# One PSUM bank for each half product of a Winograd stage in a two-layer encoder trunk

## The chip, the cores and the metric

The kernel runs on one core of one Trainium2 chip. The metric is the device time of one execution in microseconds. Five engines work side by side, each through its own instructions in order: TensorE (PE, with its weight loads shown apart as PEld), VectorE (DVE), ScalarE (ACT), GpSimd (POOL) and SyncE (SP), which issues all loads and stores here. They wait for each other through semaphores. On-chip data lies in SBUF; TensorE writes its products to PSUM, and a result is read from there by VectorE or ScalarE.

## The reference

Two layers; sequence and model width are 1024, everything is float32:

```
for l in range(DEPTH):                                   # DEPTH = 2
    h = rms_norm(x, pre_norm_g[l])
    aq, ak, av, ag, bq, bk, bv, bg = split(h @ w_in[l])  # 512,512,512,512,512,128,128,512 columns
    oa = diff_attention(aq, ak, av, lam, rel_bias)       # 4 heads, two softmaxes each, T5 bias
    ya = rms_norm(oa, diff_subln_g[l]) * (1 - lam_init) * silu(ag)
    q, k = rope(rms_norm(bq)), rope(rms_norm(bk))
    ob = gqa_attention(q, k, bv)                         # 8 query heads, 2 key/value heads of 64
    yb = ob * silu(bg)
    y = concatenate([ya, yb]) @ w_out[l]
    x = x + rms_norm(y, post_norm_g[l])
```

## The kernel before, in words

Every large product is made of three products of reduced precision: a float32 operand is split into a high part (a rounding cast, on ScalarE) and a low part (the operand less its high part, on VectorE), and high·high, high·low and low·high are added up in PSUM. "Low part" below always means that subtraction.

A layer goes through these stages. (1) The keys, values and queries of group B, then the values of group A, in chunks of token tiles (`tok_chunk`), whose results alternate between a bank of the tag `pO` and one of `pS`. In layer 0, `line` also makes the rows of the T5 bias in between, four evictions of 4x512. (2) The Winograd stage (`wino_steps`, L471 to L549): the four 512-column chunks AK, AG, BG and AQ are each computed as a 2x2 block product with seven half-size products in place of eight. `sum_steps` makes the sums of blocks of h (s1 to s4), `loads` brings four 512 KB pieces of the weight per chunk, `preps` makes the weight's seven blocks and splits them into parts. A product `i` is run in two halves `cb` of 128 columns by `run(i, cb)`: twelve matmuls of 512 columns into one PSUM bank. The list `plan` says for each product its PSUM group, which block of h it takes, whether it opens the group (`first`) or adds to what is there, and what is read from the bank afterwards: a copy to `y` tiles, an addition (`added`) of the bank to a `y` tile, or a `post` that scales, splits and stores the result (`post_parts`) or applies SiLU and stores it (`post_gate`). The kept `y` sums are called s1, u2 and u3. (3) Attention, in ticks (`tick`, L754): in each one set of scores is reduced by VectorE and exponentiated by ScalarE, the next set is computed by TensorE, older probabilities are transposed, and a piece of an older product with V is done. The last chunk's products 5 and 6 are left out of the stage and run in the first five ticks as fillers (`FILL`, L32; `fill_part`). (4) The ending (after the last scores, order `ENDING`): the remaining parts of attention, the conversions of the output weight, and the first two gated, transposed y tiles (`y_transposed`, L1009). (5) The out-projection in two halves of 512 columns, with y tiles 2 to 7 transposed on the way; then the post norm and the residual. Group A's attention is normalised on GpSimd, which also has low parts of probabilities and weights.

PSUM has eight banks: the tag `pS` has two tiles of two banks, `pT` and `pO` two tiles of one bank each. What an instruction waits for is found tile by tile: a matmul into a tile waits for every earlier reader of that tile, whichever half it read.

What sets the order: during the Winograd stage only TensorE keeps the program's order, and a scheduler places the instructions of the other engines; in attention and its ending TensorE, VectorE, ScalarE and GpSimd all keep the program's order, and SP's is the scheduler's.

In the stage before, groups a and b have one two-bank tile of `pS` for both halves, and group c one bank of `pO` for each half, in which product 6 adds to product 5. Three products lie in b (s2, s3, a22) and two in c (s1, s4).

Of the kernel before, what the change touches and what calls it, by code (L numbers as in the profile page):

```python
# [17 lines left out]
P = 128  # L18
# [35 lines left out]
def hybrid_encoder(ctx, tc, x, rel_bias, pre_norm_g, w_in, diff_lambda, diff_subln_g,  # L54
# [58 lines left out]
    def ps_o():  # L113
        return ps.tile([P, 512], F32, tag="O", name=nm("pO"), bufs=2)
# [4 lines left out]
    def f(t):  # L119
        return t.bitcast(F32)  # L120
# [105 lines left out]
    def build_bias_rows():  # L226
# [18 lines left out]
        def line(j):  # L245
            lt = e_tile()
            for i in range(2):
                pl = ps_o()
                sl = slice(i * 512, i * 512 + 512)
                pe.matmul(pl[:4], parts, ohs[j][:64, sl], start=True, stop=True)  # L250
                dve.tensor_scalar(lt[:4, sl], pl[:4], -1.0, None, ALU.mult)
# [53 lines left out]
    def layer(l, hT, ends, given):  # L305
# [164 lines left out]

        def wino_steps(c0, post):  # L471

# [19 lines left out]
            def t4():  # L492
                dve.tensor_tensor(raw[1, 0], raw[1, 0], raw[0, 0], ALU.subtract)
                parted(4, raw[1, 0])
# [3 lines left out]
            preps = [lambda: parted(0, raw[0, 0]), lambda: parted(1, raw[1, 0]), t3,  # L498
                     lambda: parted(3, raw["t3"]), t4, lambda: parted(5, raw[0, 1]), lambda: parted(6, raw[1, 1])]

            def bank(grp, cb):
                if grp == "c":
                    if (grp, cb) not in ps_:
                        ps_[grp, cb] = ps_o()
                    return ps_[grp, cb]
                if grp not in ps_:
                    ps_[grp] = ps_s()
                return ps_[grp][:, cb * 512:cb * 512 + 512]

# [24 lines left out]
            def done(cb, th, src):  # L534
# [5 lines left out]
                    ("b", "s3", False, lambda cb: added("b", "u3", "s1", cb) and None),  # L540
                    ("b", "a22", False, lambda cb: done(cb, 1, added("b", "s1", "s1", cb))),
                    ("c", "s1", True, lambda cb: done(2 + cb, 1, added("c", "u3", "u3", cb))),
                    ("c", "s4", False, lambda cb: done(2 + cb, 0, added("c", "u2", "u2", cb)))]

# [119 lines left out]
        else:  # L664
# [12 lines left out]
        chunks = [wino_steps(C_AK, post_parts(1.0, store_k)), wino_steps(C_AG, post_gate(0)),  # L677
                  wino_steps(C_BG, post_gate(1)), wino_steps(C_AQ, post_parts(-0.125, store_q))]
        loads = [fn for c in chunks for fn in c[0]]
# [7 lines left out]
        for n in range(7 * len(chunks)):  # L687
            if n < 2:
                late[n]()
            if n + WLD < len(loads):  # L690
                loads[n + WLD]()
            if n + WPR < len(preps):
                preps[n + WPR]()
            if n == 21:
                warm = s_tile()
                inorder[:] = [nc.scalar]
                act.activation(warm, neglam, AF.Exp)
                inorder[:] = [nc.tensor]
            if n < 26:
# [309 lines left out]
        def y_transposed(t):  # L1009
# [5 lines left out]
            for kh in range(2):  # L1015
# [7 lines left out]
                else:  # L1023
                    dve.tensor_tensor(gate[:, sl, :], pT, gate[:, sl, :], ALU.mult)
                split(yT[0][:, sl, :], yT[1][:, sl, :], gate[:, sl, :])
            return yT
# [214 lines left out]
```

## Time and profile before

| what | us |
|---|---|
| three runs | 1520.82, 1524.74, 1525.21 |
| median | 1524.74 |
| profiled execution | 1518.82 |
| its span | 1517.0 |
| PE, PEld busy | 1411.8, 1214.3 |
| DVE, ACT, POOL busy | 1051.1, 835.1, 662.2 |

The mean granted clock of TensorE was 0.992. Nearly all instructions are recorded through one helper, so all have line 67; they are told apart by tiles, such as `pS` or `y`. In a row of a timeline stand the start, the length, the engine, the line, the operation, what is written `<-` what is read, the count, and in brackets the idle time before it and the instruction that ended it. In a row of groups stand the total busy time and the mean length in ns, then the idle time before and its releasers.

### The profile page before, as it was taken

What the parts mean: (1) busy time and instruction counts of PE and PEld (TensorE: products, weight loads), DVE (VectorE), ACT (ScalarE), POOL (GpSimd) and SP (SyncE); (2) the same over time, 40 slices, a digit from 0 to 9 for tenths busy, and PEclk for the clock granted to TensorE, in tenths of its full rate; (3) what the DMA queues carried; (4) which work ended last, traced back from release to release, by engine and by line L of the source; (5) the groups of instructions that cost most, each with busy time, mean ns of one, the idle gap of its engine ahead of it and who ended that gap; (6) DMA issues with size and microseconds to landing.
All of it is one profiled execution on the core that took longest, in us unless ns stands there. A gap on an engine that the chain in (4) does not pass through costs nothing. (4 is left out here: it accounts for less than half of the span.)

```text
span 1517.0 us, 22632 instructions
## 1 busy us (share of the span) xinstructions
PE 1411.8 (93%) x8108; PEld 1214.3 (80%) x8108; DVE 1051.1 (69%) x1844; ACT 835.1 (55%) x1584; POOL 662.2 (44%) x708
## 2 busy tenths in 40 slices
PE   6999888888999999989999998888899999999998
PEld 6886666667999999978788876666689999998787
DVE  7869534447888888873786785434588888888624
ACT  5324233327888888853442242223488888888421
POOL 3520000006888888862233100000178888888321
PEclk9999999999999999999999999999999999999999
DMA  5467433177232323142534553224743242322223
GB/s 210 136 162 218 160 122 111 50 212 187 78 85 76 102 63 105 57 139 83 177 104 119 138 162 123 93 91 112 217 117 103 64 130 64 92 84 69 99 73 135
DMA packets 134609, 179.12 MB, mean 118 GB/s; under 512 B 10072, under 2 KB 98392, under 8 KB 132192
## 3 DMA queue, kind: packets, MB, share of 16 engines
q1 hardware_dynamic: 134496, 177.67, 38.7%
q8 instruction: 64, 1.05, 0.3%
q14 instruction: 49, 0.40, 0.1%
HBM read 120.98 MB, written 60.85 MB: 120 GB/s over the span
## 5 line engine op out<-in xcount | busy, mean ns | idle before, releaser
L67 PE MATMUL pO<-w,h 128*128 128x256 f32 (+1 forms) x3160 | 550.0, 322 | 0.0
L67 PEld LDWEIGHTS pO<-w,h 128*128 128x128 f32 x3160 | 486.2, 189 | 64.1 <-DVE y L67 0.5
L67 POOL TENSOR_SCALAR e<-e,s 128x1024 f32<-128x1024 f32 x64 | 72.1, 1127 | 559.4 <-DVE s L67 312.1
L67 PE MATMUL pS<-h,h 128*128 128x512 f32 x1024 | 295.7, 411 | 2.4 <-DVE s L67 2.4
L67 PE MATMUL pS<-h,w 128*128 128x512 f32 x768 | 189.9, 398 | 46.3 <-DVE y L67 24.0
L67 PEld LDWEIGHTS pS<-h,w 128*128 128x128 f32 x768 | 140.4, 188 | 94.5 <-DVE y L67 29.0
L67 PE MATMUL pT<-identr,e 128*128 128x128 f32 x1536 | 203.2, 275 | 7.2 <-DVE w L67 7.2
L67 PEld LDWEIGHTS pS<-h,h 128*128 128x128 f32 x1024 | 175.8, 191 | 26.5 <-issue 2.8
L67 DVE TENSOR_TENSOR w<-pT,w 128x512 fp32r<-128x512 f32 x256 | 170.1, 685 | 29.9 <-ACT w L67 29.8
L67 PEld LDWEIGHTS pT<-identr,e 128*128 128x128 f32 x1536 | 175.6, 142 | 11.4 <-issue 7.6
L67 POOL TENSOR_TENSOR w<-e,w 128x512 fp32r<-128x512 f32 x128 | 165.9, 1296 | 10.4
L67 ACT CAST w<-pT 128x512 fp32r<-128x512 f32 x256 | 143.9, 588 | 40.9 <-PE pT L67 38.0
L67 POOL TENSOR_TENSOR s<-s,mhalf 128x2 f32<-128x2 f32 (+2 forms) x96 | 85.4, 890 | 185.3 <-DVE s L67 182.0
L67 DVE TENSOR_REDUCE s<-pS 128x1 f32<-128x1024 f32 x128 | 156.3, 1221 | 10.0 <-PE pS L67 9.2
L67 ACT ACTIVATE e<-e,s 128x1024 f32<-128x1024 f32 x128 | 148.2, 1158 | 26.4 <-DVE s L67 25.7
L67 DVE CUSTOM_DVE_ANT_0 e<-pS,h 128x1024 f32<-128x1024 f32 x128 | 155.6, 1217 | 9.3 <-POOL e L67 4.4
L67 POOL TENSOR_TENSOR e<-e,e 128x1024 f32<-128x1024 f32 x64 | 153.3, 2395 | 5.3
L67 ACT ACTIVATE e<-pS,s 128x1024 f32<-128x1024 f32 x128 | 144.5, 1129 | 9.3 <-DMA h<-bq_d 5.7
L67 PE MATMUL pS<-w,h 128*128 128x512 f32 (+1 forms) x576 | 120.6, 367 | 0.0
L67 PEld LDWEIGHTS pS<-w,h 128*128 128x128 f32 x576 | 98.3, 198 | 15.5 <-issue 0.5
L67 ACT ACTIVATE e<-y 128x512 fp32r<-128x512 f32 (+2 forms) x64 | 47.3, 739 | 104.5 <-DVE y L67 77.3
L67 ACT ACTIVATE o<-pO 128x128 f32<-128x128 f32 (+2 forms) x97 | 37.0, 382 | 104.5 <-PE pO L67 93.7
(98 smaller groups left out, 1623.7 us busy)
## 6 DMA issues: line engine op xcount, KB each, us to landing
h<-aq_d SPq DMA_DIRECT2D x64, 256.0 KB, 4.3
h<-in_w_in_dram SPq DMA_DIRECT2D x20, 512.0 KB, 4.7
bq_d<-y SPq DMA_DIRECT2D x64, 128.0 KB, 2.4
av_d<-e SPq DMA_DIRECT2D x32, 256.0 KB, 2.4
e<-in_w_in_dram SPq DMA_DIRECT2D x16, 512.0 KB, 4.2
y<-in_w_in_dram SPq DMA_DIRECT2D x16, 512.0 KB, 5.2
ak_d<-e SPq DMA_DIRECT2D x32, 256.0 KB, 2.0
gate_d<-e SPq DMA_DIRECT2D x32, 256.0 KB, 2.0
```

Of the source, the lines that this page charges most:

```text
L67: ins = fn(*args, **kw)
```

## The change

Four edits. In `line`, the four evictions of 4x512 are done by ScalarE, with the scale −1, in place of VectorE. In `wino_steps` each pair of group and half has a tile of one bank: a in `pT`, b in `pS`, c in `pO`, and two new groups d and e for the products a22 and s4, in `pT` and `pS`, or for the last chunk (`tail`) both in `pO`. Products a22 and s4 each open their own group, s1 is alone in c, and what they shared in a bank is now put together on `y` tiles by one more addition per half and chunk. The order of the products is a11, a12, s2, s3, s1, a22, s4 (before: a22 ahead of s1), the weight blocks are prepared in that order, and the additions of a22 and s4 are put off to their post. So the last chunk's fillers are a22 and s4, and its last product within the stage is s1. In `y_transposed` the low parts of the y tiles are made by GpSimd, after both gate multiplications, in place of VectorE.

```
--- before.py
+++ after.py
@@ -248,7 +248,7 @@
                 pl = ps_o()
                 sl = slice(i * 512, i * 512 + 512)
                 pe.matmul(pl[:4], parts, ohs[j][:64, sl], start=True, stop=True)
-                dve.tensor_scalar(lt[:4, sl], pl[:4], -1.0, None, ALU.mult)
+                act.activation(lt[:4, sl], pl[:4], AF.Copy, scale=-1.0)
             nc.sync.dma_start(line_d[:, j * 1024:j * 1024 + 1024], lt[:4])
             if j:
                 for h in range(4):
@@ -468,7 +468,7 @@
             return [lambda: whole("s3", a21), lambda: whole("s2", a11), s1, s3s2, lambda: (s4(), parted("s2", h_tile)),
                     lambda: parted("s3", w_tile)], [lambda: parted("s1", h_tile), lambda: parted("s4", w_tile)]
 
-        def wino_steps(c0, post):
+        def wino_steps(c0, post, tail=False):
 
             raw, wb, ps_, snap = {}, {}, {}, {}
 
@@ -491,21 +491,20 @@
 
             def t4():
                 dve.tensor_tensor(raw[1, 0], raw[1, 0], raw[0, 0], ALU.subtract)
-                parted(4, raw[1, 0])
+                parted(5, raw[1, 0])
 
             loads = [lambda: load(0, 0, e_tile), lambda: load(1, 0, e_tile),
                      lambda: (load(1, 1, y_tile), load(0, 1, y_tile))] + [lambda: None] * 4
             preps = [lambda: parted(0, raw[0, 0]), lambda: parted(1, raw[1, 0]), t3,
-                     lambda: parted(3, raw["t3"]), t4, lambda: parted(5, raw[0, 1]), lambda: parted(6, raw[1, 1])]
+                     lambda: parted(3, raw["t3"]), lambda: parted(4, raw[0, 1]), t4, lambda: parted(6, raw[1, 1])]
+
+            homes = {"a": ps_t, "b": lambda: ps_s((P, 512)), "c": ps_o, "d": ps_o if tail else ps_t,
+                     "e": ps_o if tail else lambda: ps_s((P, 512))}
 
             def bank(grp, cb):
-                if grp == "c":
-                    if (grp, cb) not in ps_:
-                        ps_[grp, cb] = ps_o()
-                    return ps_[grp, cb]
-                if grp not in ps_:
-                    ps_[grp] = ps_s()
-                return ps_[grp][:, cb * 512:cb * 512 + 512]
+                if (grp, cb) not in ps_:
+                    ps_[grp, cb] = homes[grp]()
+                return ps_[grp, cb]
 
             def kept(name, cb):
                 if name not in snap:
@@ -538,9 +537,10 @@
                     ("a", "a12", False, lambda cb: done(cb, 0, bank("a", cb))),
                     ("b", "s2", True, lambda cb: added("b", "u2", "s1", cb) and None),
                     ("b", "s3", False, lambda cb: added("b", "u3", "s1", cb) and None),
-                    ("b", "a22", False, lambda cb: done(cb, 1, added("b", "s1", "s1", cb))),
-                    ("c", "s1", True, lambda cb: done(2 + cb, 1, added("c", "u3", "u3", cb))),
-                    ("c", "s4", False, lambda cb: done(2 + cb, 0, added("c", "u2", "u2", cb)))]
+                    ("c", "s1", True, lambda cb: (added("c", "u2", "u2", cb),
+                                                  done(2 + cb, 1, added("c", "s1", "u3", cb)))[1]),
+                    ("d", "a22", True, lambda cb: lambda: post(cb, 1, added("d", "u3", "u3", cb))),
+                    ("e", "s4", True, lambda cb: lambda: post(2 + cb, 0, added("e", "u2", "u2", cb)))]
 
             def run(i, cb, ks=range(4)):
                 mm(i, cb, ks)
@@ -675,7 +675,7 @@
         inorder[:] = [nc.tensor]
         early, late = sum_steps()
         chunks = [wino_steps(C_AK, post_parts(1.0, store_k)), wino_steps(C_AG, post_gate(0)),
-                  wino_steps(C_BG, post_gate(1)), wino_steps(C_AQ, post_parts(-0.125, store_q))]
+                  wino_steps(C_BG, post_gate(1)), wino_steps(C_AQ, post_parts(-0.125, store_q), True)]
         loads = [fn for c in chunks for fn in c[0]]
         preps = [fn for c in chunks for fn in c[1]]
         side = {j: [fn] for j, fn in enumerate(early)}
@@ -696,7 +696,7 @@
                 inorder[:] = [nc.scalar]
                 act.activation(warm, neglam, AF.Exp)
                 inorder[:] = [nc.tensor]
-            if n < 26:
+            if n < 7 * len(chunks) - 2:
                 for cb in range(2):
                     more = chunks[n // 7][2](n % 7, cb)
                     follow()
@@ -1022,7 +1022,10 @@
                     dve.scalar_tensor_tensor(gate[:, sl, :], pT, gsub, gate[:, sl, :], ALU.mult, ALU.mult)
                 else:
                     dve.tensor_tensor(gate[:, sl, :], pT, gate[:, sl, :], ALU.mult)
-                split(yT[0][:, sl, :], yT[1][:, sl, :], gate[:, sl, :])
+                act.copy(yT[0][:, sl, :], gate[:, sl, :])
+            for kh in range(2):
+                sl = slice(kh * 4, kh * 4 + 4)
+                gps.tensor_tensor(yT[1][:, sl, :], gate[:, sl, :], f(yT[0])[:, sl, :], ALU.subtract)
             return yT
 
         inorder[:] = [getattr(nc, n) for n in ORD]
```

Three places of the order. First TensorE in the AK chunk of layer 0, at the end of the first half of product s2 (`h209` and `h210` are the parts of s2, `w231` the weight block), its second half and the start of s3 (`w218`, `w219`). Before:

```order
L67 MATMUL pS240_1563<-h209_1347,w231_1485 128x512
L67 MATMUL pS240_1563<-h209_1347,w231_1485 128x512 [waits DVE_49]
L67 MATMUL pS240_1563<-h210_1348,w231_1485 128x512
L67 MATMUL pS240_1563<-h209_1347,w231_1485 128x512 x2
L67 MATMUL pS240_1563<-h210_1348,w231_1485 128x512
L67 MATMUL pS240_1563<-h209_1347,w231_1485 128x512 x2
L67 MATMUL pS240_1563<-h210_1348,w231_1485 128x512
L67 MATMUL pS240_1563<-h209_1347,w231_1485 128x512 x2
L67 MATMUL pS240_1563<-h210_1348,w231_1485 128x512
L67 MATMUL pS240_1563<-h209_1347,w231_1485 128x512
L67 MATMUL pS240_1563<-w218_1399,w236_1522 128x512 [waits DVE_49]
L67 MATMUL pS240_1563<-w219_1400,w236_1522 128x512
```

Now:

```order
L67 MATMUL pS241_1563<-h210_1348,w231_1485 128x512
L67 MATMUL pS241_1563<-h209_1347,w231_1485 128x512
L67 MATMUL pS243_1578<-h209_1347,w231_1485 128x512
L67 MATMUL pS243_1578<-h210_1348,w231_1485 128x512
L67 MATMUL pS243_1578<-h209_1347,w231_1485 128x512 x2
L67 MATMUL pS243_1578<-h210_1348,w231_1485 128x512
L67 MATMUL pS243_1578<-h209_1347,w231_1485 128x512 x2
L67 MATMUL pS243_1578<-h210_1348,w231_1485 128x512
L67 MATMUL pS243_1578<-h209_1347,w231_1485 128x512 x2
L67 MATMUL pS243_1578<-h210_1348,w231_1485 128x512
L67 MATMUL pS243_1578<-h209_1347,w231_1485 128x512
L67 MATMUL pS241_1563<-w218_1399,w237_1523 128x512 [waits DVE_49]
```

Before, the second half of s2 stood in the same tile and waited for VectorE's addition of the first half to `y`, and s3 waited for that of the second half. Now the second half is in a tile of its own and waits for nothing; s3's first half waits for the addition of s2's first half, a block earlier.

Second, SP between the end of the stage and the start of attention in layer 0: L943 and L946 load keys of group A and the bias, L964 loads the keys of group B (`bk_d`), L977 its values, and L563 stores queries of the AQ chunk. Before:

```order
L946 DMA h331_2428<-rep_d_79 128x1920 [waits DMAHW1_49,PE_49]
L964 DMA h332_2430<-bk_d0_92 128x2048 [waits DMAHW2_49,PE_49]
L563 DMA aq_d0_88<-e327_2394 64x4x128 [waits DMAHW3_49,Activation_49]
L563 DMA aq_d0_88<-e327_2394 64x4x128 [waits DMAHW4_49]
L563 DMA aq_d0_88<-e327_2394 64x4x128 [waits DMAHW5_49,DVE_49]
L563 DMA aq_d0_88<-e327_2394 64x4x128 [waits DMAHW6_49]
L563 DMA aq_d0_88<-e328_2414 64x4x128 [waits DMAHW7_49,Activation_49]
L563 DMA aq_d0_88<-e328_2414 64x4x128 [waits DMAHW0_49]
L563 DMA aq_d0_88<-e328_2414 64x4x128 [waits DMAHW1_49,DVE_49]
L563 DMA aq_d0_88<-e328_2414 64x4x128 [waits DMAHW2_49]
L977 DMA h333_2432<-bv_d0_93 128x2048 [waits DMAHW3_49,PE_49]
```

Now:

```order
L946 DMA h353_2458<-rep_d_79 128x1920 [waits DMAHW1_49,PE_49]
L563 DMA aq_d0_88<-e348_2422 64x4x128 [waits DMAHW2_49,Activation_49]
L563 DMA aq_d0_88<-e348_2422 64x4x128 [waits DMAHW3_49]
L563 DMA aq_d0_88<-e348_2422 64x4x128 [waits DMAHW4_49,DVE_49]
L563 DMA aq_d0_88<-e348_2422 64x4x128 [waits DMAHW5_49]
L563 DMA aq_d0_88<-e350_2444 64x4x128 [waits DMAHW6_49,Activation_49]
L563 DMA aq_d0_88<-e350_2444 64x4x128 [waits DMAHW7_49]
L563 DMA aq_d0_88<-e350_2444 64x4x128 [waits DMAHW0_49,DVE_49]
L563 DMA aq_d0_88<-e350_2444 64x4x128 [waits DMAHW1_49]
L964 DMA h354_2460<-bk_d0_92 128x2048 [waits DMAHW2_49,PE_49]
L977 DMA h355_2462<-bv_d0_93 128x2048 [waits DMAHW3_49,PE_49]
```

The load of L964 stood ahead of the eight stores and stands behind them now, next to L977; some of the stores wait for VectorE's low parts.

Third, VectorE in the ending of layer 0, around the first y tile: the gate multiplications read `pT`, the low parts write `h1247`, and `o<-o,pO` is the sum of two halves of a head pair that TensorE transposes next. Before:

```order
L67 SCALAR_TENSOR_TENSOR h1182_6444<-pT1248_6783,gsub0_665,h1182_6444 128x4x128 [waits DMAHW3_49,DMAHW6_49,DMAHW1_49,DMAHW7_49,DMAHW0_49,PE_49]
L67 TENSOR_TENSOR h1247_6782<-h1182_6444,h1247_6782 128x512 [waits DMAHW2_49,DMAHW1_49,Activation_49]
L67 TENSOR_TENSOR h1182_6444<-pT1249_6791,h1182_6444 128x4x128 [waits PE_49]
L67 TENSOR_TENSOR h1247_6782<-h1182_6444,h1247_6782 128x512 [waits Activation_49]
L67 TENSOR_TENSOR o1205_6543<-o1205_6543,pO1241_6728 64x256
L67 RECIPROCAL s1128_6173<-s1128_6173 128x4
```

Now:

```order
L67 SCALAR_TENSOR_TENSOR h1206_6476<-pT1272_6815,gsub0_665,h1206_6476 128x4x128 [waits DMAHW3_49,DMAHW6_49,DMAHW1_49,DMAHW7_49,DMAHW0_49,PE_49]
L67 TENSOR_TENSOR h1206_6476<-pT1273_6822,h1206_6476 128x4x128 [waits PE_49]
L67 TENSOR_TENSOR o1229_6575<-o1229_6575,pO1265_6760 64x256 [waits Activation_49]
L67 RECIPROCAL s1152_6205<-s1152_6205 128x4
L67 TENSOR_SCALAR y576_3456<-pO1265_6760,s1152_6205 128x64 [waits DVE_49,PE_49]
```

The two low parts have left VectorE, and the sum follows the two multiplications.

More of the change, by code (lines that the diff above doesn't have):

```diff
@@ L1024, in y_transposed @@
                     dve.tensor_tensor(gate[:, sl, :], pT, gate[:, sl, :], ALU.mult)
[L1025 removed]
+                act.copy(yT[0][:, sl, :], gate[:, sl, :])
+            for kh in range(2):
+                sl = slice(kh * 4, kh * 4 + 4)
+                gps.tensor_tensor(yT[1][:, sl, :], gate[:, sl, :], f(yT[0])[:, sl, :], ALU.subtract)
             return yT
```

31 lines of the change are left out of this document (15 added, 16 removed).

## The prediction

> **What bounds the kernel now.** I read the page's busy shares first, then the waits, then the tensor engine's timeline over the stage that the diff touches.
>
> ```profile
> PE 1411.8 (93%) x8108; PEld 1214.3 (80%) x8108; DVE 1051.1 (69%) x1844; ACT 835.1 (55%) x1584; POOL 662.2 (44%) x708
> ...
> PEld pS L67 <- DVE y L67: 47.7, 37, 2.0
> ...
> PE pS L67 <- DVE y L67: 36.7, 40, 1.6
> ```
>
> TensorE is busy 93% of the span, so 7% at most, some 105 us, can come from its idle time. The two waits are of one sort: its weight loads and its matmuls into `pS` wait 37 and 40 times for a VectorE instruction that writes a `y` tile. Those are the reads of the Winograd stage. Its timeline in layer 0 (start, length, what ran, idle time before it):
>
> ```profile
> 146.85 2.88 PE L67 MATMUL pS<-h,w 128*128 128x512 f32 x12
> 150.41 3.02 PE L67 MATMUL pS<-h,w 128*128 128x512 f32 x12 [0.68 <-ACT y L67]
> ...
> 165.05 3.06 PE L67 MATMUL pS<-h,w 128*128 128x512 f32 x12 [0.78 <-DVE y L67]
> 168.89 3.04 PE L67 MATMUL pS<-w,w 128*128 128x512 f32 x12 [0.78 <-DVE y L67]
> ...
> 184.03 5.60 PE L67 MATMUL pO<-h,w 128*128 128x512 f32 x24
> 189.47 5.60 PE L67 MATMUL pO<-w,w 128*128 128x512 f32 x24
> ...
> 324.54 3.06 PE L67 MATMUL pS<-h,w 128*128 128x512 f32 x12 [0.79 <-DVE y L67]
> 327.43 2.14 PE L67 MATMUL pS<-h,h 128*128 128x512 f32 x8
> ```
>
> In `pS` every 12 matmuls are followed by a gap, and the next 12 start 3.8 us after the last ones (165.05 to 168.89). In `pO`, where each half has a tile to itself, 24 run in one row and the next group starts 5.44 us later, so 12 matmuls cost 2.72 us where nothing is waited for. The stage holds 52 such blocks (four chunks of seven products of two halves, less the four fillers).
>
> ```profile
> 146.85:327.43 180.58, 151.26 (x625) 114.64 (x624) 80.92 (x89) 52.54 (x68) 0.00 (x0) 1.00 0.39 127
> 891.60:1072.46 180.86, 151.23 (x625) 114.64 (x624) 83.33 (x91) 53.39 (x68) 0.00 (x0) 1.00 0.35 113
> ...
> 76.00:114.00 38.00, 38.00 (x183) 31.40 (x182) 25.43 (x45) 9.80 (x18) 9.15 (x6) 1.00 0.60 160
> ```
>
> These windows (length, then busy time of PE, PEld, DVE, ACT, POOL, granted clock, DMA share, GB/s) are the stage in each layer: 180.58 and 180.86 us for 52 × 2.72 = 141.4 us of work, so 39.1 and 39.4 us are lost, 78.5 together. VectorE is busy 45% there and ScalarE 29%. The last row shows that 38 us of unbroken TensorE work kept the granted clock at 1.00, so fuller work need not lower it.
>
> **The change part by part.** *Own banks.* A block now waits only for the read of its own bank, which was written two blocks earlier, and one whole block (2.72 us) of the other half lies between. What has to fit in it is one read:
>
> ```profile
> L67 DVE TENSOR_TENSOR y<-pS,y 128x512 f32<-128x512 f32 x48 | 33.2, 691 | 82.7 <-PE pS L67 82.7
> ...
> L67 DVE SCALAR_TENSOR_TENSOR e<-y,e 128x512 fp32r<-128x512 f32 x24 | 17.7, 740 | 8.8 <-ACT e L67 8.5 <-DMA aq_d<-e 0.3
> ...
> L67 ACT COPY y<-pS 128x512 f32<-128x512 f32 x16 | 9.4, 585 | 30.1 <-PE pS L67 30.1
> ```
>
> A read with its semaphores costs 3.84 − 2.72 = 1.1 us (165.05 to 168.89), so some 1.6 us are to spare, and a read may stand behind one other VectorE instruction of 0.7 us without a stall. The gain is therefore taken whole: −78.5. The one added sum per half and chunk is 8 per layer, 8 × 0.69 = 5.5 us of VectorE. Stage time falls to some 141 us, VectorE's load to (81 + 5.5)/141 = 61%; that the work hides is covered by TensorE's 141 us. The exception is a read behind a weight part of 1.2 us and a sum of 0.7; I allow 0 to 6 us over both layers and take +3.
>
> *The queue of loads at the start of attention.* In the order before, SP issues the load of the first BK tile (L964) ahead of the eight stores of the AQ chunk's last post (L563); now it stands behind them (the rows of SP's order, above). Those stores wait for VectorE's low part of the last half.
>
> ```profile
> 312.27 0.60 SPq L964 DMA_DIRECT2D h<-bk_d  x1
> 325.22 6.43 SPq L563 DMA_DIRECT2D aq_d<-e  x8
> 331.75 0.57 SPq L977 DMA_DIRECT2D h<-bv_d  x1
> ...
> 331.46 1.07 PE L67 MATMUL pS<-h,h 128*128 128x512 f32 x4
> ...
> h<-bk_d SPq DMA_DIRECT2D x1, 1024.0 KB, 12.0
> h<-bv_d SPq DMA_DIRECT2D x1, 1024.0 KB, 6.1
> ```
>
> The last block of the stage ends at about 327.4, where the first scores begin. The BV load, next in the queue behind the same stores, is issued 4.4 us later; the extra sum adds 0.6, so BK will leave 5.0 us after the stage's end. It is as large as BV, which landed after 6.1 us; the BK of before took 12.0 in a crowd of loads. So it lands 11 to 17 us after the end, and the third score set, the first that reads BK (331.46 above), wants it 4.1 us after. Everything behind it on TensorE waits too, since matmuls run in program order. I take 11, as the crowd is over by then: 6.9 us of waiting (bounds 4 and 13). After such a gap TensorE is slow for a while:
>
> ```profile
> 345.75 1.29 PE L67 MATMUL pT<-identr,e 128*128 128x128 f32 x8
> 348.22 1.17 PE L67 MATMUL pS<-h,h 128*128 128x512 f32 x4 [1.18 <-DVE s L67]
> 352.47 1.94 PE L67 MATMUL pT<-identr,e 128*128 128x128 f32 x8 [3.09 <-DVE w L67]
> 354.06 2.06 PE L67 MATMUL pS<-h,h 128*128 128x512 f32 x4
> ```
>
> After 3.09 us idle, eight transposes took 1.94 and four matmuls 2.06 us against 1.29 and 1.17 just before: some 2.4 us lost with the next group. Against that the two gaps in these rows, 4.3 us, come from VectorE running late, and while TensorE waits for BK it catches up; I credit 1.8. Per layer 6.9 + 2.4 − 1.8 = 7.5, for two layers +15 (bounds 8 and 26; layer 1 has the same order of its loads). The Trainium skill, "TensorE: Matmul & The Clock Gate", section "Part 1: The HAM clock gate", says that an idle window of about 3.4 us halves the clock until about 3.4 us of activity; by that the slow spell would cost 1.7 rather than 2.4 us, and the sum would be 1.4 us lower.
>
> *Fillers.* a22 and s4 each open their own bank, so the second no longer waits for the other's sum; before, such waits in the first ticks are not visible as TensorE gaps. Taken as nothing; cover is the score sets between them.
>
> *Bias lines.* Four evictions leave VectorE, whose backlog delayed a bias matmul in layer 0 only:
>
> ```profile
> 133.88 0.40 PE L67 MATMUL pO<-e,rbs 64*4 64x512 f32 x1 [1.98 <-DVE e L67]
> ```
>
> At best these 1.98 us and a little behind them go, at worst nothing does, if other VectorE work fills the place: −2, bounds −3 and 0.
>
> *Low parts of y on GpSimd.* Only the ending of each layer's attention can feel it, since the out-projection behind runs without gaps. VectorE there, TensorE and GpSimd:
>
> ```profile
> 655.88 0.69 DVE L67 TENSOR_TENSOR h<-h,h 128x512 fp32r<-128x512 f32 x1 [0.69 <-ACT h L67]
> 656.49 0.68 DVE L67 TENSOR_TENSOR h<-pT,h 128x512 f32<-128x512 f32 x1
> 657.86 0.72 DVE L67 TENSOR_TENSOR h<-h,h 128x512 fp32r<-128x512 f32 x1 [0.69 <-ACT h L67]
> 658.60 0.42 DVE L67 TENSOR_TENSOR o<-o,pO 64x256 f32<-64x256 f32 x1
> ...
> 659.17 0.41 PE L67 MATMUL pO<-identr,o 128*128 128x128 f32 x2 [3.37 <-DVE o L67]
> ...
> 663.98 0.62 POOL L67 CAST w<-e 128x512 fp32r<-128x512 f32 x1 [0.97 <-ACT e L67]
> ...
> 665.93 3.41 POOL L67 TENSOR_TENSOR w<-h,w 128x1024 fp32r<-128x1024 f32 x1
> ...
> L67 POOL TENSOR_TENSOR w<-e,w 128x512 fp32r<-128x512 f32 x128 | 165.9, 1296 | 10.4
> ```
>
> TensorE waits 3.37 us for the sum at 658.60, which stands behind two low parts with two waits for ScalarE: 2 × 0.69 + 2 × 0.69 = 2.8 us go. GpSimd gets two sums of about 1.30 us ahead of the cast at 663.98, which has 0.97 us free, so the last probabilities come some 1.7 us later while TensorE needs them earlier; that gives 1 to 3 us back. The first out-projection tiles wait for GpSimd's low parts in place of VectorE's. Net −2.5 per layer, −5 for both; bounds −10 and +4. By the Trainium skill, "SBUF — State Buffer", section "Who interferes with whom", a VectorE instruction with two SBUF inputs locks out a GpSimd read; GpSimd's 3.41 us above, beside VectorE's low parts, bear that out. If each moved sum were held up by one VectorE instruction of 0.69 us, the two at the start would cost 1.4 us a layer more, and the sum would be 2.8 us higher.
>
> Sum: −78.5 + 3 + 15 − 2 − 5 = −67.5 us. The profiled execution took 1518.82 us (span 1517.0 and 1.8 around it): 1451.3. The median of the runs, 1524.74, is 5.9 above that execution, so I forecast 1457 for the median.
>
> **The rivals.** *BK is hidden after all.* If the load leaves earlier, or lands in less than 6 us while the first two score sets and the fillers stretch, the +15 falls away: 1442. For it: VectorE also runs late there; against it: the order of the queue. *VectorE becomes the stage's bound.* Sums, low parts and weight differences would come in bursts; reads behind two 1.2 us instructions would stall TensorE, and half of the 78.5 stays: 1496. For it: VectorE's 36 us in 38 of the window just ahead of the stage:
>
> ```profile
> 114.00:152.00 38.00, 34.27 (x140) 26.44 (x139) 36.31 (x38) 16.99 (x21) 0.00 (x0) 0.96 0.74 221
> ```
>
> against it: 45% in the stage itself. *The change does not do what it says*: a block is still held to the previous one by something else, such as the sum of a shared `y` tile or an evicted bank that is read late, and only the small terms are left: 1524.7 + 15 − 2 − 5 = 1533, or 1518 without the BK wait; about 1525. *Slower*: the weight loads. A shorter stage has to bring the same four 512 KB loads per chunk, whose `e` and `y` buffers come free with the posts, two of which are now deferred. If the four came one behind another after the last post, at 4.2 and 5.2 us each in the page's rows of loads, 18.8 us a chunk, 150 over eight, the kernel would take 1457 + 150 = 1607; it decides from (1524.7 − 1457)/8 = 8.5 us a chunk.
>
> ```profile
> e<-in_w_in_dram SPq DMA_DIRECT2D x16, 512.0 KB, 4.2
> y<-in_w_in_dram SPq DMA_DIRECT2D x16, 512.0 KB, 5.2
> ```
>
> Against it: DMA share 0.35 to 0.39 in the stage, and each load is issued four products ahead of its use.
>
> **How the numbers follow.** Forecast 0.60; BK hidden 0.15; VectorE as the bound 0.15; no effect 0.05; slower 0.05. 1457 is the likeliest case. Its own range, from the terms' bounds all at once, is 1441 to 1482: −78.5 + 0 + 8 − 3 − 10 = −83.5 and −78.5 + 6 + 26 − 0 + 4 = −42.5 from 1524.7. The range of 8 in 10 goes from 1438 to 1488, for the first rival below and part of the second above. A measurement tells about 0.3%, 4.6 us, from no change; only half of the no-effect case lies within that, and the rest on either side: faster 0.92, same 0.03, slower 0.05.
>
> **What would show it.** Own banks: in the stage the rows of x12 with gaps become unbroken rows of x24 or more, the stage's windows are 141 to 145 us in each layer, and the wait of `pS` for VectorE's `y` falls from 36.7 to under 5 us. BK: a gap of 5 to 9 us at the third score set, released by the load of `h` from `bk_d`, with a granted clock below 0.9 behind it, in both layers. Ending: the 3.37 us gap falls to under 1 us, with a new wait for GpSimd of 1 to 3 us within 15 us of it. Bias: the 1.98 us gap is gone. The prediction is wrong if the stage stays above 160 us, or if it falls to 141 and the time does not.

## The result, and the profile after

| | before | changed |
|---|---|---|
| median of the runs, us | 1522.78 (4 runs, 1520.6 to 1525.21) | 1441.36 (4 runs, 1440.87 to 1443.26) |
| profiled execution, us | 1518.82 | 1443.26 |
| its span, us | 1517.0 | 1441.4 |

The ratio is 0.9467, with a 95% interval of 0.9447 to 0.9488: 81 us less. The forecast was 1457 (1438 to 1488). The changed kernel's TensorE in the stage of layer 0 and behind it, from its timeline (start, length, what ran, idle time before it):

```profile
145.42 11.04 PE L67 MATMUL pT<-h,w 128*128 128x512 f32 x48
156.30 5.60 PE L67 MATMUL pS<-h,w 128*128 128x512 f32 x24
161.74 5.60 PE L67 MATMUL pS<-w,w 128*128 128x512 f32 x24
...
281.42 5.60 PE L67 MATMUL pO<-h,w 128*128 128x512 f32 x24
286.86 1.98 PE L67 MATMUL pS<-h,h 128*128 128x512 f32 x8
288.67 2.20 PE L67 MATMUL pO<-h,w 128*128 128x512 f32 x9
297.29 2.05 PE L67 MATMUL pS<-h,h 128*128 128x512 f32 x4 [6.42 <-issue]
299.13 3.25 PE L67 MATMUL pO<-h,w 128*128 128x512 f32 x9
...
314.35 1.17 PE L67 MATMUL pS<-h,h 128*128 128x512 f32 x4
317.95 1.72 PE L67 MATMUL pT<-identr,e 128*128 128x128 f32 x8 [2.44 <-DVE w L67]
```

Four blocks, 48 matmuls, now run in one row, and no gap is left between 145.42 and 286.86. The wait of `pS` for VectorE's `y`, 36.7 us before, no longer appears among TensorE's waits. Then comes the new gap of 6.42 us. Windows of the two stages, of the gap and of the 6 us behind it (length, busy time of PE, PEld, DVE, ACT and POOL, granted clock, DMA share, GB/s):

```profile
145.42:286.86 141.44, 141.44 (x626) 117.12 (x624) 84.71 (x97) 53.86 (x68) 0.00 (x0) 1.00 0.48 155
853.10:994.62 141.52, 141.52 (x625) 116.96 (x624) 86.20 (x98) 53.81 (x68) 0.00 (x0) 1.00 0.42 135
...
291.00:297.00 6.00, 0.00 (x0) 0.00 (x0) 1.08 (x2) 3.65 (x5) 0.00 (x0) 0.79 0.92 294
297.00:303.00 6.00, 5.71 (x17) 4.56 (x18) 2.53 (x3) 1.73 (x3) 0.00 (x0) 0.64 0.82 253
```

TensorE is busy in the whole of each stage, and the clock stays at 1.00 there; behind the gap it is 0.64. SP's timeline around the gap, and the landing time of the load in it:

```profile
276.72 0.54 SPq L946 DMA_DIRECT2D h<-rep_d  x1
286.37 5.30 SPq L563 DMA_DIRECT2D aq_d<-e  x8
291.76 0.56 SPq L964 DMA_DIRECT2D h<-bk_d  x1
...
h<-bk_d SPq DMA_DIRECT2D x1, 1024.0 KB, 5.4
```

The profile gives the gap's releaser only as "issue", but BK was issued at 291.76 and took 5.4 us, which ends at 297.2, where the third score set starts.

The whole span, cut at the same instructions of TensorE in every profile: the stage's first matmul, the first scores, the first product of probabilities with V (256 columns), and the first transposes of a y tile. Both layers are added up; the last column but one holds the ending, the out-projection and what follows.

| kernel | start | stages | first ticks | rest of attention | ending and behind | span |
|---|---|---|---|---|---|---|
| before | 146.85 | 361.44 | 61.24 | 591.42 | 356.05 | 1517.0 |
| changed | 145.42 | 282.96 | 74.02 | 590.53 | 348.47 | 1441.4 |
| bk_early | 143.82 | 282.88 | 61.36 | 591.87 | 348.47 | 1428.4 |
| banks_only | 146.70 | 282.87 | 78.55 | 590.52 | 358.66 | 1457.3 |
| two_bank_tiles | 143.82 | 340.46 | 58.58 | 592.38 | 348.46 | 1483.7 |
| old_plan | 143.83 | 282.88 | 77.27 | 590.51 | 348.41 | 1442.9 |
| y_low_dve | 143.83 | 282.88 | 73.20 | 590.53 | 357.56 | 1448.0 |
| lines_dve | 145.08 | 282.88 | 73.56 | 590.54 | 348.44 | 1440.5 |
| sums_x2 | 143.76 | 284.07 | 70.51 | 590.53 | 348.43 | 1437.3 |
| sums_x3 | 143.69 | 296.01 | 74.52 | 590.82 | 350.46 | 1455.5 |
| y0_late | 143.87 | 282.88 | 61.72 | 591.39 | 346.54 | 1426.4 |
| low_later | 143.69 | 282.89 | 62.47 | 593.10 | 346.55 | 1428.7 |

Of the 75.6 us between the two spans, the stages give 78.5, the endings 7.6, the start 1.4 and the rest of attention 0.9, and the first ticks take 12.8 back. The first ticks and the rest of attention belong together: in the five kernels whose first ticks take less than 63 us, the rest takes 0.9 to 2.6 us longer than the 590.5 of most others.

The ending of layer 0, TensorE and GpSimd in the changed kernel:

```profile
621.09 0.44 PE L67 MATMUL pO<-identr,o 128*128 128x128 f32 x2 [0.51 <-DVE o L67]
...
627.92 0.66 PE L67 MATMUL pT<-identr,y 128*128 128x128 f32 x4 [0.64 <-DVE w L67]
...
633.36 1.09 PE L67 MATMUL pO<-w,h 128*128 128x256 f32 x7 [0.96 <-POOL w L67]
...
624.55 3.52 POOL L67 TENSOR_TENSOR h<-h,h 128x512 fp32r<-128x512 f32 x2
628.03 3.37 POOL L67 TENSOR_TENSOR w<-h,w 128x1024 fp32r<-128x1024 f32 x1
```

The wait of 3.37 us is down to 0.51, and GpSimd now releases one of 0.96.

### The profile page after: what moved, and what is told of

Its sections match the earlier page's. It is cut to its first block, busy times and chain, and to the rows that moved or that the text cites. A ratio compares the mean times of both kernels' runs of the same rounds, so it can differ in the third digit from the quotient of the medians.

```text
span 1441.4 us, 22677 instructions
## 1 busy us (share of the span) xinstructions
PE 1392.2 (97%) x8108; PEld 1218.6 (85%) x8108; DVE 1036.9 (72%) x1824; ACT 837.2 (58%) x1588; POOL 697.9 (48%) x740
## 4 chain that ended last, share of the span: by engine, by line
PE 70%; DVE 3%; POOL 2%; issue 2%; DMA 1%; ACT 1%; SPq 0%; POOLq 0%; DVEq 0%; ACTq 0%
PE pO L67 30%; PE pS L67 23%; PE pT L67 16%; DVE y L67 1%; POOL w L67 1%; DMA aq_d<-e 0%; POOL h L67 0%; POOL e L67 0%; SPq L563 0%; DVE s L67 0%; ACT e L67 0%; DVE h L67 0%; DVE e L67 0%; DVE w L67 0%; POOL s L67 0%
## 5 line engine op out<-in xcount | busy, mean ns | idle before, releaser
L67 PE MATMUL pS<-h,h 128*128 128x512 f32 x1024 | 297.6, 413 | 12.8 <-issue 12.8
L67 POOL TENSOR_TENSOR s<-s,mhalf 128x2 f32<-128x2 f32 (+2 forms) x96 | 81.8, 852 | 189.2 <-DVE s L67 185.9
L67 ACT CAST w<-pT 128x512 fp32r<-128x512 f32 x256 | 143.7, 587 | 41.5 <-PE pT L67 38.6
L67 PE MATMUL pT<-h,w 128*128 128x512 f32 x528 | 122.0, 389 | 0.0
L67 PEld LDWEIGHTS pT<-h,w 128*128 128x128 f32 x528 | 99.1, 188 | 20.6
```

Source lines behind the costliest of these rows:

```text
L67: ins = fn(*args, **kw)
```

## The experiments

The theory: the gain is that a block waits only for its own bank; the order of SP's queue costs the 12.8 us; GpSimd's part is worth what the ending gained. The rivals: the new groups and order make the gain; VectorE is what is late behind the stage.

**bk_early.** The three helper functions that issue attention's first loads are moved up, their three calls ahead of attention go, and

```
+            if n == 25:
+                state.update(q=load_q(0, 0), ak=load_ak(0), bk=load_bk(0))
             if n < 7 * len(chunks) - 2:
```

> The changed kernel, with the first loads of attention (queries, keys and bias of group A, keys of group B) issued in the program ahead of the AQ chunk's last product, so that on SP the load of BK stands ahead of the eight stores again. Theory (the order of SP's queue makes the wait of 6.4 us): the gap at the third score set is gone in both layers, the first stretch of attention takes 30 to 31 us in each layer as it did before the change (36.4 and 37.6 with it), and the time is 1441.4 - 12.8 = 1428.6 us (1428 to 1431). Rival (VectorE, with one more sum per half, is late there anyway): the gap only moves to the next transposes and less than half is gained, 1436 us or more.

Measured: 1430.58 us (1430.17 to 1431.83), ratio to the kernel before 0.9414 (0.94 to 0.9428). Its SP and its TensorE in layer 0:

```profile
275.75 0.68 SPq L705 DMA_DIRECT2D h<-bk_d  x1
284.77 5.31 SPq L563 DMA_DIRECT2D aq_d<-e  x8
```

```profile
287.07 2.20 PE L67 MATMUL pO<-h,w 128*128 128x512 f32 x9
289.38 1.20 PE L67 MATMUL pS<-h,h 128*128 128x512 f32 x4
290.41 2.23 PE L67 MATMUL pO<-h,w 128*128 128x512 f32 x9
...
306.16 1.20 PE L67 MATMUL pS<-h,h 128*128 128x512 f32 x4 [1.32 <-DVE s L67]
310.50 1.82 PE L67 MATMUL pT<-identr,e 128*128 128x128 f32 x8 [3.14 <-DVE w L67]
```

The third score set (289.38) starts without the gap, and the first ticks are back at 61.36 us against 61.24 before the change: the 12.7 us there hung on the place of one load in a queue. Both waits for VectorE (1.32 and 3.14 us) stand there again, as in the kernel before; the changed kernel has only one of 2.44. The spans of the two profiles are 13.0 us apart, the medians 10.8, each beside its own runs of the kernel before. Of the 13.0, 1.6 lie at the start, which this edit does not touch (the profiled execution of the changed kernel has a slow spell there, a few us at a lower granted clock; see lines_dve), and the rest of attention takes 1.3 back (in layer 0 with a wait of 0.79 us for VectorE at 321.34). So the load's place is worth about 11.4 us in all. This kernel beats the changed one, with nothing else altered.

**banks_only.** The kernel before, with

```
-                if grp == "c":
-                    if (grp, cb) not in ps_:
-                        ps_[grp, cb] = ps_o()
-                    return ps_[grp, cb]
-                if grp not in ps_:
-                    ps_[grp] = ps_s()
-                return ps_[grp][:, cb * 512:cb * 512 + 512]
+                if (grp, cb) not in ps_:
+                    ps_[grp, cb] = {"a": ps_t, "b": lambda: ps_s((P, 512)), "c": ps_o}[grp]()
+                return ps_[grp, cb]
```

> The kernel before with one edit: groups a and b have a one-bank tile for each half (a in pT, b in pS), c as it was. The products keep their old order and groups (s2, s3, a22 in b; s1, s4 in c), no sum is added, bias lines and low parts of y stay on VectorE. Theory (a read may lag one block as soon as the halves have tiles of their own): the stage takes 141 to 143 us in each layer; BK stands behind the stores here too, so its wait stays; 1441.4 + 7.6 (ending) + 1.4 (lines) = 1450 us (1447 to 1455). Rival (the new groups for a22 and s4 carry the gain): the stage stays above 155 us and the time above 1480 us.

Measured: 1458.4 us (1455.62 to 1459.39), ratio 0.9593 (0.9578 to 0.9607). The stage:

```profile
146.70:288.14 141.44, 141.44 (x626) 117.12 (x625) 79.94 (x89) 53.02 (x68) 0.00 (x0) 1.00 0.48 154
```

The stage is as short as with the whole change, so the rival of the new groups falls for the stage. The time is 3 us above the expected range: the endings differ from the changed kernel's by 10.2 us rather than 7.6, and the first ticks by 4.5, which nothing in the expectation held. The endings of the kernel before have the same waits of 3.37 us, but behind them eight matmuls (`pO<-w,h`) take 1.20 us in layer 0 and 2.06 in layer 1; here they take 2.06 in both.

**old_plan** asks whether those 4.5 us are the new groups. The changed kernel with

```
-                    ("c", "s1", True, lambda cb: (added("c", "u2", "u2", cb), ...
-                    ("d", "a22", True, lambda cb: lambda: post(cb, 1, added("d", "u3", "u3", cb))),
-                    ("e", "s4", True, lambda cb: lambda: post(2 + cb, 0, added("e", "u2", "u2", cb)))]
+                    ("b", "a22", False, lambda cb: done(cb, 1, added("b", "s1", "s1", cb))),
+                    ("c", "s1", True, lambda cb: done(2 + cb, 1, added("c", "u3", "u3", cb))),
+                    ("c", "s4", False, lambda cb: done(2 + cb, 0, added("c", "u2", "u2", cb)))]
```

and the weight blocks in the old order.

> The changed kernel with the order of products, their groups and the weight order of before (s2, s3, a22 add up in b; s1, s4 in c; one sum less per half), but one bank for each half as in the change; bias lines and low parts of y as in the change. BK stands behind the stores, as in the change. Theory (the new groups are worth little in the stage, and a few us in the first ticks of attention, where s4's half no longer waits for the sum of s1's in the same bank): the stage is 141.4 us in both layers, the first stretch of attention takes 38.5 and 40.0 us as in banks_only against 36.4 and 37.6, the time is 1441.4 + 4.5 = 1446 us (1444 to 1448). Rival (the new groups do nothing; banks_only lost its 8 us elsewhere): 1440 to 1443 us.

Measured: 1445.11 us (1444.49 to 1447.4), ratio 0.951 (0.9483 to 0.9537). First ticks of layer 0:

```profile
294.84 2.05 PE L67 MATMUL pS<-h,h 128*128 128x512 f32 x4 [5.36 <-issue]
...
313.57 1.16 PE L67 MATMUL pS<-h,h 128*128 128x512 f32 x4 [1.18 <-DVE s L67]
317.79 1.97 PE L67 MATMUL pT<-identr,e 128*128 128x128 f32 x8 [3.06 <-DVE w L67]
```

The wait for BK is 1.1 us shorter (5.36 against 6.42). Of this, 0.6 is the earlier issue of the load, 4.3 us after the stage's end against 4.9, which fits the one sum less that VectorE has ahead of the stores. But both later waits for VectorE are there at full length, while the changed kernel has only one of 2.44. The new groups and order together thus give 3.3 us in the first ticks (77.27 to 74.02) and nothing in the stage. The other 1.3 us of banks_only's 4.5 stay open.

**two_bank_tiles.** The changed kernel with a and b in shared tiles again:

```
+                if grp in "ab":
+                    if grp not in ps_:
+                        ps_[grp] = ps_s()
+                    return ps_[grp][:, cb * 512:cb * 512 + 512]
                 if (grp, cb) not in ps_:
```

and e in `ps_o`.

> The changed kernel, with groups a and b back in one two-bank tile of pS for both halves; c, d, e one bank per half (e in pO), new order, new groups and the other edits kept. BK stands ahead of the stores here. Theory (own banks make the gain): 32 blocks per layer wait for the block before again, at 39.1/40 = 0.98 us each as before, 31.3 us a layer; no wait for BK: 1441.4 + 62.6 - 12.8 = 1491 us (1480 to 1500), the stage 170 to 175 us. Rival (the new order and groups make it): the stage stays near 142 us and the time is 1429 to 1441 us.

Measured: 1486.69 us (1485.58 to 1487.43), ratio 0.9783 (0.9767 to 0.98).

```profile
162.03 3.04 PE L67 MATMUL pS<-h,w 128*128 128x512 f32 x12 [0.78 <-DVE y L67]
165.85 3.03 PE L67 MATMUL pS<-w,w 128*128 128x512 f32 x12 [0.78 <-DVE y L67]
...
143.82:313.09 169.27, 148.75 (x626) 115.25 (x624) 84.90 (x97) 53.91 (x68) 0.00 (x0) 1.00 0.42 135
```

The waits of 0.78 us are back where a tile is shared, at the same cadence of 3.8 us as before the change, and 57.5 us of the stages' 78.5 are lost again (282.96 to 340.46; 62.6 was expected). The gain is the tiles'.

**sums_x2 and sums_x3** ask how near the edge the reads now are. In bk_early,

```
-                dve.tensor_tensor(dst, bank(grp, cb), kept(base, cb), ALU.add)
+                for _ in range(2):          # 3 in sums_x3
+                    dve.tensor_tensor(dst, bank(grp, cb), kept(base, cb), ALU.add)
```

> The kernel of bk_early with every addition of a PSUM bank to a y tile issued twice in a row on VectorE (the second one writes the same place; sums made in place take the bank twice, so the outputs are not the reference's). It asks how much slack a read has. Theory (a read has 1.6 us to spare and VectorE 38.1 - 21.7 us in most chunks): 12 more additions of 0.69 us are 8.3 us a chunk; the second and third chunk hide them, the first one (VectorE 30.8 of 38.1 us before) is just full and loses 1 to 3 us; the stage takes 142 to 145 us in each layer, and with 1 to 3 us more in the first ticks of attention the time is 1433 to 1441 us. Rival (the reads are already on the edge): each doubled read stalls TensorE, the stage takes 150 us or more and the time is above 1447 us.

> As sums_x2, with each addition issued three times (outputs not the reference's). Theory: 24 more additions are 16.6 us a chunk; VectorE has 30.8 + 16.6 = 47 us of work in the first chunk against 38.1, so it is the bound there, and 38 in the second and third, so the slack is used up: stage 150 to 160 us in each layer, time 1450 to 1475 us. Rival (only the latency of a single read counts, not VectorE's load): the first addition behind a block still comes in time and the stage stays below 146 us.

Measured: 1438.34 us (1437.46 to 1439.08) and 1456.21 us (1454.88 to 1458.55). The first and the second chunk of the stage with two sums:

```profile
143.76:181.90 38.14, 38.14 (x170) 31.61 (x169) 33.07 (x42) 14.22 (x18) 0.00 (x0) 1.00 0.63 201
181.90:220.00 38.10, 38.10 (x170) 31.58 (x169) 31.09 (x40) 14.84 (x19) 0.00 (x0) 1.00 0.40 145
```

and the stage with three:

```profile
163.41 3.01 PE L67 MATMUL pS<-w,w 128*128 128x512 f32 x12 [0.52 <-DVE y L67]
...
143.69:291.70 148.01, 143.44 (x626) 116.59 (x624) 133.42 (x178) 50.93 (x66) 0.00 (x0) 1.00 0.46 152
```

With two sums the stage takes 142.03 us against 141.44: a read may be twice as long at almost no cost, so at least 0.7 us of the 1.6 us of slack in the prediction are there. That all 1.6 are is not shown: three sums add 1.4 us to a read, and gaps appear, but VectorE's load has grown as well. With three, VectorE is busy 133 of 148 us and the stage grows by 6.6 us a layer, to 2 us less than the expected range began with, and above the rival's 146. What the doubling costs lies nearly all in the first ticks (70.51 against 61.36), where 1 to 3 us were expected, so the time lies in the expected range for another reason than the theory's. TensorE now waits 2.15 us for VectorE ahead of the third score set (291.96 in layer 0): that is the place where VectorE has no slack.

**y_low_dve.** The changed kernel with the low parts of y back on VectorE, between the gate multiplications:

```
-                act.copy(yT[0][:, sl, :], gate[:, sl, :])
-            for kh in range(2): ...
-                gps.tensor_tensor(yT[1][:, sl, :], gate[:, sl, :], f(yT[0])[:, sl, :], ALU.subtract)
+                split(yT[0][:, sl, :], yT[1][:, sl, :], gate[:, sl, :])
```

> The changed kernel with the low parts of the y tiles back on VectorE, directly behind each gate multiplication. Theory (the two low parts held up the sum that TensorE waits for): the gap of 3.4 us ahead of the transposes of the head pair comes back in both layers and so do the small ones at the next y tile; 1441.4 + 7.6 = 1449 us (1447 to 1450). Rival (GpSimd's lateness takes back what VectorE gains, and the ending got shorter for another reason): 1440 to 1444 us.

Measured: 1450.76 us (1449.74 to 1452.66), ratio 0.9547 (0.9532 to 0.9561).

```profile
622.00 0.41 PE L67 MATMUL pO<-identr,o 128*128 128x128 f32 x2 [3.37 <-DVE o L67]
...
632.88 0.66 PE L67 MATMUL pT<-identr,y 128*128 128x128 f32 x4 [0.85 <-DVE h L67]
```

The wait is back at 3.37 us to the digit, and the endings take 9.1 us more than with GpSimd (357.56 against 348.47). The time lies 0.8 us above the expected range, which added the 7.6 us of the kernel before. Here eight matmuls behind the wait take 1.92 and 2.06 us, so both layers have a slow spell, while the kernel before has one in layer 1 alone. GpSimd's part of the change is worth 7.6 us against the kernel before and 9.1 against this one.

**y0_late** asks what GpSimd's lateness gives back. In bk_early, the first y tile's low parts go to VectorE one tick later:

```
+            if t == 0:
+                after(0, lambda: low(dve))
+            else:
+                low(gps)
```

> The kernel of bk_early with the low parts of the first y tile back on VectorE, but issued a tick later, behind the sum of the head pair; y tiles 1 to 7 stay on GpSimd. Theory (GpSimd's 3.5 us for them push the weight part and the last probabilities, which TensorE then waits for): the gap of 0.96 us that GpSimd releases and those of 0.6 and 0.4 us before it shrink, 1 to 2 us a layer, 1430.6 - 3 = 1427.5 us (1426.5 to 1429.5). Rival (VectorE's 1.4 us just push the same chain): no change, 1430 to 1432 us.

Measured: 1428.23 us (1428.2 to 1428.33), ratio 0.9401 (0.9387 to 0.9415), the fastest kernel here; bk_early's median was 1430.58 beside other runs of the kernel before, and the intervals of the two ratios overlap, so the difference rests on the traces. In these the endings shrink from 348.47 to 346.54 us, and in layer 0

```profile
617.29 1.26 PE L67 MATMUL pT<-identr,e 128*128 128x128 f32 x8 [0.59 <-DVE w L67]
...
625.18 1.20 PE L67 MATMUL pO<-w,h 128*128 128x256 f32 x8
...
618.23 3.44 POOL L67 TENSOR_TENSOR w<-h,w 128x1024 fp32r<-128x1024 f32 x1
```

the product that waited 0.96 us for GpSimd (625.18) no longer waits, while a new wait of 0.59 us for VectorE appears. So GpSimd's lateness cost about 1 us a layer, not the 1 to 3 of the prediction.

**lines_dve.** The changed kernel with

```
-                act.activation(lt[:4, sl], pl[:4], AF.Copy, scale=-1.0)
+                dve.tensor_scalar(lt[:4, sl], pl[:4], -1.0, None, ALU.mult)
```

> The changed kernel with the four evictions of the bias rows back on VectorE. Theory (they stand in VectorE's backlog ahead of the low parts that the bias products wait for): the gaps at the two second bias products grow from 0.83 and 0.88 to 1.08 and 1.98 us and the stage begins 1.4 to 3 us later (at 146.7 to 146.9 against 143.8 to 145.4), time 1441.4 + 2 = 1443.4 us (1442.5 to 1445). Rival: other VectorE work fills the place, the stage begins at the same time and the time is 1441 us.

Measured: 1443.7 us (1442.28 to 1446.03), 2.3 us above the changed kernel's median, with overlapping runs. The profiled execution is 0.9 us shorter than the changed kernel's. The second bias products, here (with the 24 matmuls behind the later one), then in the changed kernel, and last those 24 matmuls in the kernel before:

```profile
119.99 0.40 PE L67 MATMUL pO<-e,rbs 64*4 64x512 f32 x1 [1.08 <-DVE e L67]
133.77 0.39 PE L67 MATMUL pO<-e,rbs 64*4 64x512 f32 x1 [1.98 <-DVE e L67]
134.09 5.71 PE L67 MATMUL pS<-w,h 128*128 128x512 f32 x24
```

```profile
121.39 0.40 PE L67 MATMUL pO<-e,rbs 64*4 64x512 f32 x1 [0.84 <-ACT e L67]
134.07 0.39 PE L67 MATMUL pO<-e,rbs 64*4 64x512 f32 x1 [0.88 <-ACT e L67]
```

```profile
134.21 7.37 PE L67 MATMUL pS<-w,h 128*128 128x512 f32 x24
```

The two gaps differ by 1.34 us together; the last read waited for is now ScalarE's. The stage begins at 145.08, and at 143.7 to 143.9 in eight profiles with the bias lines on ScalarE, so the difference is that of the gaps, 1.2 to 1.4 us. Two more profiles with them on VectorE, before and banks_only, begin at 146.85 and 146.70: behind the same gap of 1.98 us the next 24 matmuls take 7.37 and 7.35 us there and 5.71 here. The changed kernel's own start, 145.42, holds a slow spell of the same size far ahead of the bias products: behind a gap of 1.81 us at 41 us, its granted clock from 41 to 49 us was 0.79. In bk_early the same gap stands there, and the clock was 1.00. So the term is 1.3 us, and up to 3 where a slow spell follows the gap.

**low_later** tries for the waits that are left in the first ticks. In y0_late, the low part of each filler's post is put off by one more tick:

```
+                def low():
                     dve.scalar_tensor_tensor(o[:, 1], src, scale, f(o)[:, 0], ALU.mult, ALU.subtract)
                     store(cb, th, f(o))
+                if held_back:               # set at the start of attention to: after(1, fn)
+                    held_back[0](low)
+                else:
+                    low()
```

> The kernel of y0_late with the low part (and the stores) of each filler's post issued one tick later than its sum and its cast. In the first ticks VectorE stands idle 2.27, 1.24, 0.78 and 1.23 us ahead of those low parts because ScalarE's cast is late, and TensorE then waits 1.3 and 3.1 us for VectorE and is slow behind that. Theory (VectorE's queue is held up by those low parts): both gaps and the slow spell shrink, 2 to 6 us a layer: 1428.2 - 8 = 1420 us (1416 to 1425). Rival (VectorE's work itself is too much in these ticks): no change, 1427 us or more.

Measured: 1431.47 us (1430.55 to 1434.64), 3 us more than y0_late. VectorE in these ticks:

```profile
300.69 0.68 DVE L67 SCALAR_TENSOR_TENSOR e<-y,e 128x512 fp32r<-128x512 f32 x1
304.73 1.22 DVE L67 CUSTOM_DVE_ANT_0 e<-pS,h 128x1024 f32<-128x1024 f32 x1 [3.36 <-PE pT L67]
```

VectorE no longer waits ahead of the low parts, but it waits 3.36 us ahead of the next reduction, for transposes on TensorE, and that reduction starts 0.2 us earlier than it did (304.91 in y0_late), as much as the first scores do. TensorE's second wait for VectorE shrinks from 3.15 to 1.89 us, but a new one of 1.58 us for ScalarE follows (315.25), and the rest of attention takes 1.7 us more, which stays open. So moving the low parts out of the way did not free VectorE's queue, and the theory is wrong. The reduction writes an `e` tile, and the transposes are the last readers of the tile that it takes over; that the `e` tiles are the bound there follows from the names, and was not tried.

## Why the prediction was right, and where it was off

*Own banks:* right. 78.48 us gained in the stages against 78.5 in the sum. The +3 us allowed for reads behind other work was not needed; sums_x2 shows that even a doubled read costs only 0.6 us a layer. That fuller work keeps the clock at 1.00, which rested on one window of 38 us, held over two windows of 141 us.

*The queue of loads:* right, with its place, cause and size. The gap was forecast at 6.9 us and is 6.42 and 6.39; BK was to land 11 us after the stage's end and landed 10.3 after it (286.86 to 297.2). The net was put at +15 and measured +12.8. Of the 2.2 us between them 1.0 is the gaps, and the rest, by subtraction, the slow spells: 2.4 us a layer were allowed, and they come to about 1.8.

*The credit and the fillers:* right in size, wrong in cause. The prediction credited 1.8 us a layer because VectorE would catch up while TensorE waits for BK, and took the new groups as nothing. The waits for VectorE did shrink by 1.83 and 1.85 us (4.27 to 2.44 in layer 0). But in old_plan TensorE waits 5.36 us for BK and they stay at 1.18 and 3.06, and in bk_early, with the new groups and no wait for BK, they are 1.32 and 3.14. Only both together shorten them, so the size was in part luck. Beside the wait for BK the new groups and order are worth 3.3 us in the first ticks (old_plan); without it bk_early shows no gain (61.36 against 61.24 before). Perhaps the place of the fillers' sums in VectorE's queue decides this; it was not tried.

*Bias lines:* −2 stood in the sum; the gaps shrink by 1.3 us. The gap of 1.98 us is not gone, as the prediction had it: 0.88 us for ScalarE's read are left.

*The ending:* the mechanism was right, the term too small: −5 in the sum, −7.6 measured between the two profiles and 9.1 against y_low_dve. The 2.8 us for the two low parts was right (3.37 to 0.51). The net of −2.5 a layer does not follow from the prediction's own pieces: 2.8 less the 1 to 3 given back is −1.8 to +0.2, and with that the forecast would have been some 3 us further off. Two pieces were mis-sized: GpSimd's lateness was put at 1 to 3 us a layer and is about 1, and the small gaps at the next y tile (0.84 and 0.55 us) and the slow spell that followed the 3.37 us gap in layer 1 were left out of the net value.

*From the profile to the median:* the largest miss, and not one of the kernel. 5.9 us were added because the profiled execution of before lay that far under the median of its three runs. Three later series of before have medians of 1519.3 to 1520.6, only 0.5 to 1.8 above it, so most of the 5.9 belongs to that one series. The changed kernel's median lies 1.9 us under its profiled execution, which holds the slow spell of 1.6 us at its start. Of the 16 us between 1457 and 1441, 8 are this step; the other 8 are +3 of reads, 2.2 of the first ticks, 2.6 of the endings and 0.9 of the rest of attention, less 0.6 of the start.

*The rivals:* "BK is hidden" did not happen, and bk_early shows what it would have given: 1430.6, where the prediction had 1442. VectorE as the stage's bound is refuted by the stage of 141.44 us and by sums_x2; with sums_x3, where VectorE is busy 133 of 148 us, TensorE waits for it again. The late weight loads, the rival on the slower side, did not show: no gap in the stage waits for a load.

## What to carry to other kernels

Where every group of matmuls is followed by a gap as long as one read, and another group with a tile for each half shows none, the shared tile is the likely cost; here the gaps added up to 78.5 us and 78.48 were gained. When work is moved ahead of a queue's loads, look at the order of that queue itself: here one load behind eight stores cost 12.7 us in the first ticks, a sixth of the gain, and moving three calls in the program gave all but about 1.3 of it back. A gap can cost more than its length, since the instructions behind it may run slowly. Whether they do differs between executions (5.71 or 7.37 us for 24 matmuls behind the same 1.98 us), so its price is read from the rows after it too.

## What the runs showed of the hardware

Behind the 6.42 us gap the granted clock was 0.64 over 6 us, and a set of four score matmuls took 2.05 in place of 1.07 us. This agrees with the Trainium skill, "TensorE: Matmul & The Clock Gate", section "Part 1: The HAM clock gate", which has the clock fall after an idle window of about 3.4 us; but the rows of before show the same slowness (1.94 and 2.06 us) behind gaps of only 1.18 and 3.09 us, and the changed kernel shows it (1.72 for eight transposes, 2.06 us for four score matmuls) behind one of 2.44. No run here shows a length of gap from which it sets in.

GpSimd and VectorE slow each other down in the ending: GpSimd's two low parts took 3.52 us there (624.55, above), and its weight part 3.37 (628.03), while in the same kernel a few us later stand

```profile
633.26 2.39 POOL L67 TENSOR_TENSOR w<-h,w 128x1024 fp32r<-128x1024 f32 x1
635.61 2.55 POOL L67 TENSOR_TENSOR h<-h,h 128x512 fp32r<-128x512 f32 x2
...
624.85 2.09 DVE L67 TENSOR_TENSOR w<-h,w 128x1024 fp32r<-128x1024 f32 x1 [0.87 <-POOL w L67]
627.84 1.32 DVE L67 TENSOR_TENSOR w<-h,w 128x1024 fp32r<-128x1024 f32 x1
```

Beside the two slow ones stand VectorE's own weight parts, with both inputs in SBUF, and the first of these is slow itself (2.09 against 1.32 us); beside the two later ones VectorE has no such instruction. For the two low parts that is 1.0 us, where the prediction's estimate had 1.4.

In y0_late the weight part still takes 3.44 us with the low parts gone, beside VectorE's own weight part (618.19, 1.22 us), so the low parts are not needed for it.
